# Conv taps as diagonal products, short convolutions' middle tap on ScalarE, decay masks added by TensorE

## The chip, the cores and the metric

The kernel runs on one core of one Trainium2 chip. The metric is the device time of one launch in microseconds (us). The engines are called TensorE (PE in the profile, its weight loads PEld), VectorE (DVE), ScalarE (ACT), GpSimd (POOL) and SyncE (SP, which issues most transfers). All engines take their own instructions in order and wait for each other through semaphores.

## What is computed

Two layers over 256 latent tokens and 256 context tokens of width 1024 (each layer two feed-forward parts around a mixer), then two further layers on the 256 latent tokens alone. The change touches only the first layer's "even" mixer. Cut to what matters:

```python
qkv, z, ab, glu = split(h @ w_in)                     # 512 tokens in all, latent and context
qkv = silu(depthwise_conv(qkv, qkv_conv))             # 5 taps, 1536 channels
q, k, v = split(qkv)                                  # 4 heads of 128 each
g, beta = gates(ab)                                   # per direction, token and head
# gated delta rule in both directions; within a chunk:
gcum  = cumsum(g)
decay = where(tril, exp(gcum[i] - gcum[j]), 0)        # upper triangle in the other direction
m     = strict(beta * k k^T * decay);  a = I + m      # triangular solve against v and k
attn  = tril(q k^T * decay)
val, gate = split(glu)
y = depthwise_conv(val * sigmoid(gate), dw_conv) + dw_bias   # 31 taps, 512 channels
y = silu(layer_norm(y))
out = concat(rms_norm(o) * silu(z), y) @ w_out
```

## The kernel before, in words

Nearly all weight products are made exact enough by splitting both operands into a high and a low part of a faster 32-bit form (`hi`, line 77, on ScalarE; `lo`, line 80, on VectorE) and adding three products (`mm3`, lines 111 to 113). Products that are not split are in plain F32: scores of keys and queries, state products, level products of the triangular inverse, the attention scores of the second layer (line 1153).

The mixer is `even` (lines 558 to 845) and `even_scan` (847 to 1046), then `mix_even`, the output product. `even` goes through the input projection in blocks of 128 channels by 512 tokens (`blocks`: 24 products into one of two banks of PSUM): gates and keys (four blocks, each with `conv5`, sum of squares and a transpose), decay tiles, inverse of the diagonal blocks, the gated input of the long convolution (stage `e_glu`, lines 782 to 795: four padded blocks `upad`), queries, values, and the `z` gate. Between blocks `ada_next` inserts one group of a conditioning product (line 229, whose weights come straight from memory). `even_scan` completes the inverse by levels (lines 861 to 902), steps the state over four token tiles in two directions (`step`), merges the directions (`merge`), does the long convolution (`conv31`, lines 998 to 1007) and its layer norm (`cnorm`).

Nothing fixes the order by hand: a planner orders the instructions of each engine by the order of the program text as priority, by readiness in its own estimate of time, and by free buffers. So instructions that stand late in the text, such as the taps of `conv31`, run early where their engine would be free. Tiles with the same tag share a fixed number of buffers, and a new one waits until the old one's last reader is done.

The places that the change and the prediction touch:

- `conv5` (line 593): ScalarE copies the product from its bank into a padded tile (597); VectorE multiplies by the first tap (602) and adds four more (604); ScalarE applies SiLU (607). It runs twelve times.
- Decay tiles (lines 730 to 750): for each of four token tiles and two directions, four transposes of a broadcast gate column (740) into a bank of role `ch` (two banks), each followed by a Relu on ScalarE (741), then one Exp (742), a multiply by a triangular mask of ones and zeros on VectorE (744), four multiplies (747) into a tile `un` (two buffers), which is stored to memory (749).
- `e_glu`: product of the gate block, sigmoid into the padded tile (791), product of the value block, multiply on VectorE (793).
- `conv31` for each of four blocks: the first tap with the bias (1005) and 30 further taps (1007), all on VectorE, into `y`.
- Bank 7 (role `pss`) holds the sums of squares, first of the keys, later of the queries.
- `un`, `pad`, `acc` live in the pool `ip`, which is freed after `even`; `upad`, `dm` and `y` live on.

Of the kernel before, what the change touches and what calls it, by code (L numbers as in the profile page):

```python
# [9 lines left out]
F32 = mybir.dt.float32  # L10
F32R = mybir.dt.float32r
I32 = mybir.dt.int32
AF = mybir.ActivationFunctionType
ALU = mybir.AluOpType
# [7 lines left out]
LN_EPS = 1e-5  # L22
RMS_EPS = 1e-6
NEG = -1.0e30


def shape_constants():
# [26 lines left out]
class Net:  # L54
# [503 lines left out]
    def even(self, xh, xl):  # L558
        nc, I = self.nc, self.I
        v = nc.vector  # L560
        W = I["even_w_in"][0].rearrange("(k p) n -> p k n", p=128)
        gd, ip = self.gd, self.ip
        qT = gd.tile([128, 4, 512], F32, name="qT")
        kT = gd.tile([128, 4, 512], F32, name="kT")
        y = self.yo.tile([128, 4, 512], F32, name="y")
# [5 lines left out]
        cw = self.cw  # L571

        def unit(c0):
            raw = self.raw()
            rv = raw.rearrange("p (k n) -> p k n", k=KC)
            nc.sync.dma_start(rv, W[:, :, c0:c0 + 256])
            return [self.split(rv[:, 4 * q:4 * q + 4, :]) for q in range(2)]

        def blocks(todo, cuts=((0, 512),)):

            out = [self.pt() for _ in todo]
            for a, b in cuts:
                for ps, lhs in zip(out, todo):
                    for k in range(KC):
                        wh, wl = lhs(k)
                        self.mm3(ps[:, a:b], wh, wl, xh[:, k, a:b], xl[:, k, a:b], k == 0, k == KC - 1)
            return out

        def col(pieces, j):
            c = slice(128 * j, 128 * j + 128)  # L590
            return lambda k: (pieces[k // 4][0][:, k % 4, c], pieces[k // 4][1][:, k % 4, c])

        def conv5(ps, blk, out=None):
            pad = ip.tile([128, 2, 260], F32, name="pad", tag="pad", bufs=2)
            nc.gpsimd.memset(pad[:, :, 0:2], 0.0)
            nc.gpsimd.memset(pad[:, :, 258:260], 0.0)
            nc.scalar.copy(pad[:, :, 2:258], ps.rearrange("p (s t) -> p s t", s=2))
            acc = ip.tile([128, 2, 256], F32, name="acc", tag="acc", bufs=3)
            for j in range(5):
                w = cw[:, 12 * j + blk:12 * j + blk + 1]  # L600
                if j == 0:
                    v.tensor_scalar(acc, pad[:, :, 0:256], w, None, op0=ALU.mult)
                else:
                    v.scalar_tensor_tensor(acc, pad[:, :, j:j + 256], w, acc, op0=ALU.mult, op1=ALU.add)
            fa = acc.rearrange("p s t -> p (s t)")
            out = fa if out is None else out
            nc.scalar.activation(out, fa, AF.Silu)
            return out
# [27 lines left out]
        ps, psk = blocks([lambda k: (wh[:, k, :], wl[:, k, :]), col(pieces, 0)], ((0, 256), (256, 512)))  # L636
        abf = ip.tile([128, 512], F32, name="abf", tag="acc", bufs=3)[:16]
        nc.scalar.copy(abf, ps[:16])
        ps = self.pt([128, 4, 16], "ch")
# [10 lines left out]
        def small(name, pool=None):  # L650
            return (pool or gd).tile([128, 2, 4, 4], F32, name=name)
# [7 lines left out]
        xa, ax, u, den, s, s2, g = (small(n, ip) for n in ("ga", "gx", "gu", "gn", "gs", "gt", "gg"))  # L659
# [31 lines left out]
        ps = self.pt([128, 64], "ch")  # L691
# [3 lines left out]
        gc, egc, negc, etail, egl = (small(n) for n in ("gc", "egc", "negc", "etail", "egl"))  # L695
# [11 lines left out]
        for h in range(4):  # L707
            if h == 2:
                pieces = unit(768)
            if h:  # L710
                psk, = blocks([col(pieces, h % 2)])
            c = conv5(psk, 4 + h)
            sumsq(c, h, pss)
            tokmajor(c, khat[:, :, h, :])
            if h % 2:
                self.ada_next()
        rk = gd.tile([128, 16], F32, name="rk")
        self.rsqrt(rk, pss.rearrange("p t h -> p (t h)"), 1e-6)
        for t in (2, 3, 0, 1):
            v.tensor_mul(khat[:, t], khat[:, t], rk[:, 4 * t:4 * t + 4, None].to_broadcast([128, 4, 128]))  # L720
            nc.sync.dma_start(kvd[t, :, 0], khat[:, t])
            ps = self.pt([128, 4, 128], "tp")
# [4 lines left out]
        self.mark("e_dm")  # L727

        dm = {}
        for t in (2, 3, 0, 1):  # L730
            ts = slice(128 * t, 128 * (t + 1))
            psg = self.pt([128, 4, 128], "tp")
            for h in range(4):
                nc.tensor.matmul(psg[:, h, :], kT[:, h, ts], kT[:, h, ts], start=True, stop=True)
            for d in range(2):
                psr = self.pt([128, 4, 128], "ch")
                e = gd.tile([128, 4, 128], F32, name="dm", tag="dm", bufs=8)
                for h in range(4):
                    cl = gc[:, d, t, h:h + 1]
                    nc.tensor.transpose(psr[:, h, :], cl.to_broadcast([128, 128]), self.ident)  # L740
                    nc.scalar.activation(e[:, h, :], psr[:, h, :], AF.Relu, scale=-1.0, bias=cl)
                nc.scalar.activation(e, e, AF.Exp, scale=-1.0)
                m = (self.le, self.ge)[d]
                v.tensor_mul(e, e, m[:, None, :].to_broadcast([128, 4, 128]))
                un = ip.tile([128, 4, 128], F32, name="un", tag="un", bufs=2)
                for h in range(4):
                    v.scalar_tensor_tensor(un[:, h, :], psg[:, h, :], nbeta[:, d, t, h:h + 1], e[:, h, :],
                                           op0=ALU.mult, op1=ALU.mult)
                nc.sync.dma_start(ud[d][4 * t:4 * t + 4].rearrange("h j i -> j h i"), un)
                dm[d, t] = e  # L750
# [3 lines left out]
        for d in range(2):  # L754
            z = gd.tile([128, 16, 128], F32, name=f"Z{d}")
# [27 lines left out]
        for b2 in range(2):  # L783
            pv, pg = unit(2064 + 256 * b2), unit(2576 + 256 * b2)
            for j in range(2):
                pad = gd.tile([128, 2, 286], F32, name=f"upad{2 * b2 + j}")
                nc.gpsimd.memset(pad[:, :, 0:15], 0.0)
                nc.gpsimd.memset(pad[:, :, 271:286], 0.0)
                psg, = blocks([col(pg, j)])
                core = pad[:, :, 15:271]  # L790
                nc.scalar.activation(core, psg.rearrange("p (s t) -> p s t", s=2), AF.Sigmoid)
                psv, = blocks([col(pv, j)])
                v.tensor_mul(core, core, psv.rearrange("p (s t) -> p s t", s=2))
                pads.append(pad)
                self.ada_next()

        self.mark("e_q")
# [2 lines left out]
        for h in range(4):  # L800
            if h % 2 == 0:
                pieces = unit(128 * h)
            ps, = blocks([col(pieces, h % 2)])
            conv5(ps, h, qT[:, h, :])
            sumsq(qT[:, h, :], h, pss)
            if h % 2:
                self.ada_next()
# [3 lines left out]
        for t in (2, 3, 0, 1):  # L811
            ts = slice(128 * t, 128 * (t + 1))
            ps = self.pt([128, 4, 128], "tp")
# [7 lines left out]
        for h in range(4):  # L821
            if h % 2 == 0:
                pieces = unit(1024 + 128 * h)
            ps, = blocks([col(pieces, h % 2)])
            c = conv5(ps, 8 + h)
            vt = ip.tile([128, 4, 128], F32, name="vt", tag="acc", bufs=3)
            tokmajor(c, vt)
            nc.sync.dma_start(kvd[:, :, 1, h, :].rearrange("t p c -> p t c"), vt)
            if h % 2:
                self.ada_next()  # L830
# [3 lines left out]
        for h in range(4):  # L834
            if h % 2 == 0:
                pieces = unit(1536 + 128 * h)
            ps, = blocks([col(pieces, h % 2)])
# [9 lines left out]
    def even_scan(self, E):  # L847


        nc = self.nc  # L850
        v = nc.vector
# [6 lines left out]
        y = E["y"]  # L858
# [139 lines left out]
        def conv31(b):  # L998
            self.mark("e_cf")
            acc = y[:, b, :].rearrange("p (s t) -> p s t", s=2)  # L1000
            pad = E["pads"][b]
            for i in range(31):
                w = self.dw[:, 4 * i + b:4 * i + b + 1]
                if i == 0:
                    v.tensor_scalar(acc, pad[:, :, 0:256], w, self.cf_bias[:, b:b + 1], op0=ALU.mult, op1=ALU.add)
                else:
                    v.scalar_tensor_tensor(acc, pad[:, :, i:i + 256], w, acc, op0=ALU.mult, op1=ALU.add)  # L1007


        def cnorm():  # L1010
# [30 lines left out]
        for b in range(4):  # L1041
            conv31(b)
# [221 lines left out]
    def hybrid(self, l, xs, last):  # L1264
# [3 lines left out]
        with tc.tile_pool(name="hb", bufs=1, reuse_waits="tile") as hb:  # L1268
# [10 lines left out]
            for i in (0, 2):  # L1279
                v.tensor_scalar(negc[:, i], self.ge, -NEG, NEG, op0=ALU.mult, op1=ALU.add)  # L1280
            causal = [negc[:, 0], negc[:, 1:3].rearrange("p a b -> p (a b)")]
# [75 lines left out]
            def select():  # L1357

                for t in range(2):
# [21 lines left out]
                    for i in range(8):  # L1381
                        v.max(m8, idx)
                        v.match_replace(idx, m8, idx, 3.0 * NEG)
                        yield
                    v.tensor_scalar(idx, idx, 2.0 * NEG, None, op0=ALU.is_le)
                    v.tensor_scalar(idx, idx, -NEG, NEG, op0=ALU.mult, op1=ALU.add)
                    v.tensor_tensor(idx, idx, causal[t], op=ALU.min)
# [418 lines left out]
```

## Time and profile before

| | |
|---|---|
| median of 3 runs | 2521.53 us (2517.78 to 2525.92) |
| the profiled execution | 2521.85 us |
| its span, first to last instruction | 2520.1 us |
| mean granted TensorE clock | 0.997 of full speed |
| even mixer with its output product | about 430 to 745 us of the span |

The profile gives for each engine its busy time, for groups of instructions their count and mean duration, and for idle time what ended it. A matmul's end is modelled, and neighbouring matmuls overlap in the record, so a busy TensorE need not be at its limit. Rows of stretches (windows) give the busy time of each engine between two times. In the timeline consecutive equal instructions are merged into one row, with their count.

### The profile page before, as it was taken

Reading aid. Unit: us, or ns where it says so; the run is one execution under the profiler, and the core shown is the slowest. Engines: PE = TensorE matmul, PEld = TensorE weight load, DVE = VectorE, ACT = ScalarE, POOL = GpSimd, SP = SyncE. Lnnn points to the kernel's source line nnn. Section 1 sums busy time; section 2 is a strip of 40 time slices with the busy share of each in tenths; the row PEclk is TensorE's granted clock in tenths of the full one; section 3 lists DMA queues with packets and bytes.
Section 4 is the critical chain, followed back from the end, with each engine's and each line's share of the span. In section 5 each row is a group of like instructions: output and inputs, shape, how many; then the busy total and the mean of one; then the engine's idle time right before and its main releaser. Section 6 shows DMA issues by size and latency. Waiting matters only on the chain.

```text
span 2520.1 us, 32989 instructions
## 1 busy us (share of the span) xinstructions
PE 2458.2 (98%) x13096; PEld 2003.7 (80%) x13096; DVE 1382.8 (55%) x2430; ACT 1049.0 (42%) x1764; POOL 38.2 (2%) x102
## 2 busy tenths in 40 slices
PE   7999999999999999999999999999999999999998
PEld 4777887767888888888788887589978878888776
DVE  3322245799887322346222346665576766657755
ACT  3322234723334222324222335654455564546544
POOL 0000001000000000000000000000000000000000
PEclk9999999999999999999999999999999999999999
DMA  8644333566535333225443324767655335553353
GB/s 281 215 150 134 134 101 134 170 204 235 199 110 193 91 100 101 101 95 189 154 130 100 118 97 167 275 205 214 192 175 181 102 134 192 176 172 113 126 180 142
DMA packets 342728, 395.76 MB, mean 157 GB/s; under 512 B 19464, under 2 KB 236845, under 8 KB 342573
## 3 DMA queue, kind: packets, MB, share of 16 engines
q1 hardware_dynamic: 342573, 393.64, 47.7%
q8 instruction: 103, 1.69, 0.3%
q14 instruction: 52, 0.43, 0.0%
HBM read 377.06 MB, written 16.55 MB: 156 GB/s over the span
## 4 chain that ended last, share of the span: by engine, by line
PE 74%; issue 13%; DVE 8%; DMA 2%; ACT 2%; POOL 1%; SPq 0%; DVEq 0%; POOLq 0%; ACTq 0%
PE b L111 21%; PE b L112 21%; PE b L113 21%; PE b L229 2%; PE b L301 1%; DVE wlo L80 1%; DVE y L1007 1%; PE b L1352 1%; DMA fraw<-in_ada_w 1%; DVE st L435 1%; DVE b L433 1%; PE b L1161 1%; DVE x L441 0%; DVE x L434 0%; PE b L235 0%
## 5 line engine op out<-in xcount | busy, mean ns | idle before, releaser
L80 DVE TENSOR_TENSOR wlo<-wraw,whi 128x1024 fp32r<-128x1024 f32 (+2 forms) x499 | 600.1, 1206 | 689.0 <-ACT whi L77 687.9
L77 ACT CAST whi<-wraw 128x1024 fp32r<-128x1024 f32 (+2 forms) x499 | 514.7, 1038 | 499.3 <-PE b L112 288.9
L111 PE MATMUL b<-xh,whi 128*128 128x512 f32 (+1 forms) x1688 | 607.3, 360 | 4.2 <-ACT xh L77 3.9
L113 PE MATMUL b<-xh,wlo 128*128 128x512 f32 (+1 forms) x1688 | 605.2, 359 | 3.1 <-DVE wlo L80 3.1
L112 PE MATMUL b<-xl,whi 128*128 128x512 f32 (+1 forms) x1688 | 606.7, 360 | 0.4 <-DVE xl L80 0.2
L111 PEld LDWEIGHTS b<-xh,whi 128*128 128x128 f32 x1688 | 319.6, 189 | 66.2 <-issue 10.9
L113 PEld LDWEIGHTS b<-xh,wlo 128*128 128x128 f32 x1688 | 320.1, 190 | 50.5 <-DVE wlo L80 4.8
L112 PEld LDWEIGHTS b<-xl,whi 128*128 128x128 f32 x1688 | 320.0, 190 | 46.8 <-issue 1.7
L111 PE MATMUL b<-whi,hh 128*128 128x512 f32 x652 | 254.5, 390 | 0.0
L113 PE MATMUL b<-whi,hl 128*128 128x512 f32 x652 | 254.3, 390 | 0.0
L112 PE MATMUL b<-wlo,hh 128*128 128x512 f32 x652 | 254.3, 390 | 0.0
L465 ACT ACTIVATE h<-b 128x512 f32<-128x512 f32 (+1 forms) x88 | 47.8, 544 | 321.1 <-PE b L113 321.0
L111 PE MATMUL b<-whi,x 128*128 128x512 f32 (+1 forms) x448 | 171.3, 383 | 0.8 <-ACT xtt L308 0.8
L113 PE MATMUL b<-whi,x 128*128 128x512 f32 (+1 forms) x448 | 171.1, 382 | 0.0
L112 PE MATMUL b<-wlo,x 128*128 128x512 f32 (+1 forms) x448 | 170.6, 381 | 0.0
L111 PEld LDWEIGHTS b<-whi,hh 128*128 128x128 f32 x652 | 122.4, 188 | 26.3
L113 PEld LDWEIGHTS b<-whi,hl 128*128 128x128 f32 x652 | 122.4, 188 | 26.1
L112 PEld LDWEIGHTS b<-wlo,hh 128*128 128x128 f32 x652 | 122.4, 188 | 25.9
L80 DVE TENSOR_TENSOR hl<-h,hh 128x512 fp32r<-128x512 f32 (+1 forms) x81 | 50.2, 621 | 150.3 <-ACT hh L77 150.3
L77 ACT CAST hh<-h 128x512 fp32r<-128x512 f32 (+1 forms) x81 | 45.9, 567 | 196.8 <-PE b L112 188.0
L111 PEld LDWEIGHTS b<-whi,x 128*128 128x128 f32 x448 | 84.2, 188 | 16.2 <-ACT xtt L308 1.0
L112 PEld LDWEIGHTS b<-wlo,x 128*128 128x128 f32 x448 | 84.2, 188 | 16.0 <-issue 1.5
(475 smaller groups left out, 3181.9 us busy)
## 6 DMA issues: line engine op xcount, KB each, us to landing
wraw<-in_ffn_w_gu SPq DMA_DIRECT2D x170, 512.0 KB, 4.8
fraw<-in_ada_w SPq DMA_DIRECT2D x64, 1024.0 KB, 6.4
wraw<-in_w_in SPq DMA_DIRECT2D x64, 1024.0 KB, 4.9
wraw<-in_ffn_w_down SPq DMA_DIRECT2D x44, 1024.0 KB, 4.8
wraw<-in_even_w_in SPq DMA_DIRECT2D x12, 1024.0 KB, 5.1
wraw<-in_w_branch SPq DMA_DIRECT2D x12, 1024.0 KB, 4.8
araw<-in_ada_w SPq DMA_DIRECT2D x8, 1024.0 KB, 7.9
xd<-x SPq DMA_DIRECT2D x16, 512.0 KB, 4.3
```

What stands on the lines that cost most here:

```text
L77: self.nc.scalar.copy(out, in_)
L80: return self.nc.vector.tensor_sub(out, in_, hi)
L111: mm(ps, ah, bh, start=start, stop=False)
L112: mm(ps, ah, bl, start=False, stop=False)
L113: mm(ps, al, bh, start=False, stop=stop)
L229: nc.tensor.matmul(ps[32 * q:32 * q + 32], self.sil[:, 4 * u + q, :], raw[:, q, :], start=(u == 0), stop=(u == 1))
L301: nc.tensor.transpose(ps[:, j, :], n[:, 128 * k:128 * (k + 1)], self.ident)
L433: nc.vector.tensor_mul(ys[n], ys[n], gate[:, c])
L435: nc.vector.bn_stats(st[:, n, :], x[:, c])
L465: nc.scalar.activation(h(c), ps[0], AF.Silu)
L1007: v.scalar_tensor_tensor(acc, pad[:, :, i:i + 256], w, acc, op0=ALU.mult, op1=ALU.add)
L1161: nc.tensor.matmul(po, vt[:, c, h // 4], pT[:, c], start=(c == 0), stop=(c == 3))
```

## The change

Three edits, all in the even mixer:

1. `conv5`: the middle tap (2) is made by ScalarE from the bank, as a copy with a per-channel scale straight into `acc`; VectorE adds the other four taps. The padded copy stays.
2. Decay tiles: two small tiles `low` (0 where the mask was one, -1e30 where it was zero) are made once. For each decay tile TensorE first writes the identity times the broadcast `low` over the whole bank and then adds the gate columns with four plain products in place of the transposes. Relu and Exp turn the masked places into zeros, so the multiply by the mask goes.
3. Long convolution: in `e_glu`, as soon as a padded block is there, ScalarE makes six diagonal matrices (identity times the tap's per-channel weight), in buffers of the tag `un`; TensorE adds up six products of a diagonal with the shifted block in bank 7; ScalarE writes the sum plus bias into `y`. `conv31` adds the other 25 taps on VectorE.

```diff
@@ -22,6 +22,7 @@
 LN_EPS = 1e-5
 RMS_EPS = 1e-6
 NEG = -1.0e30
+PT = 6
 
 
 def shape_constants():
@@ -596,12 +597,10 @@
             nc.gpsimd.memset(pad[:, :, 258:260], 0.0)
             nc.scalar.copy(pad[:, :, 2:258], ps.rearrange("p (s t) -> p s t", s=2))
             acc = ip.tile([128, 2, 256], F32, name="acc", tag="acc", bufs=3)
-            for j in range(5):
-                w = cw[:, 12 * j + blk:12 * j + blk + 1]
-                if j == 0:
-                    v.tensor_scalar(acc, pad[:, :, 0:256], w, None, op0=ALU.mult)
-                else:
-                    v.scalar_tensor_tensor(acc, pad[:, :, j:j + 256], w, acc, op0=ALU.mult, op1=ALU.add)
+            w = lambda j: cw[:, 12 * j + blk:12 * j + blk + 1]
+            nc.scalar.activation(acc, ps.rearrange("p (s t) -> p s t", s=2), AF.Copy, scale=w(2))
+            for j in (0, 1, 3, 4):
+                v.scalar_tensor_tensor(acc, pad[:, :, j:j + 256], w(j), acc, op0=ALU.mult, op1=ALU.add)
             fa = acc.rearrange("p s t -> p (s t)")
             out = fa if out is None else out
             nc.scalar.activation(out, fa, AF.Silu)
@@ -727,6 +726,10 @@
         self.mark("e_dm")
 
         dm = {}
+        low = ip.tile([128, 2, 128], F32, name="low").rearrange("p d f -> d p f")
+        low = [low[d] for d in range(2)]
+        for z, m in zip(low, (self.le, self.ge)):
+            v.tensor_scalar(z, m, -NEG, NEG, op0=ALU.mult, op1=ALU.add)
         for t in (2, 3, 0, 1):
             ts = slice(128 * t, 128 * (t + 1))
             psg = self.pt([128, 4, 128], "tp")
@@ -735,13 +738,17 @@
             for d in range(2):
                 psr = self.pt([128, 4, 128], "ch")
                 e = gd.tile([128, 4, 128], F32, name="dm", tag="dm", bufs=8)
+
+                nc.tensor.matmul(psr, self.ident, low[d][:, None, :].to_broadcast([128, 4, 128]),
+                                 start=True, stop=False)
                 for h in range(4):
                     cl = gc[:, d, t, h:h + 1]
-                    nc.tensor.transpose(psr[:, h, :], cl.to_broadcast([128, 128]), self.ident)
+                    nc.tensor.matmul(psr[:, h, :], cl.to_broadcast([128, 128]), self.ident,
+                                     start=False, stop=(h == 3))
+                for h in range(4):
+                    cl = gc[:, d, t, h:h + 1]
                     nc.scalar.activation(e[:, h, :], psr[:, h, :], AF.Relu, scale=-1.0, bias=cl)
                 nc.scalar.activation(e, e, AF.Exp, scale=-1.0)
-                m = (self.le, self.ge)[d]
-                v.tensor_mul(e, e, m[:, None, :].to_broadcast([128, 4, 128]))
                 un = ip.tile([128, 4, 128], F32, name="un", tag="un", bufs=2)
                 for h in range(4):
                     v.scalar_tensor_tensor(un[:, h, :], psg[:, h, :], nbeta[:, d, t, h:h + 1], e[:, h, :],
@@ -792,6 +799,17 @@
                 psv, = blocks([col(pv, j)])
                 v.tensor_mul(core, core, psv.rearrange("p (s t) -> p s t", s=2))
                 pads.append(pad)
+
+                b = 2 * b2 + j
+                dg = [ip.tile([128, 4, 128], F32, name="dg", tag="un", bufs=2) for _ in range(0, PT, 4)]
+                dg = [dg[i // 4][:, i % 4] for i in range(PT)]
+                ps = self.pt([128, 2, 256], bank=7)
+                for i in range(PT):
+                    nc.scalar.activation(dg[i], self.ident, AF.Copy, scale=self.dw[:, 4 * i + b:4 * i + b + 1])
+                for i in range(PT):
+                    nc.tensor.matmul(ps, dg[i], pad[:, :, i:i + 256], start=(i == 0), stop=(i == PT - 1))
+                nc.scalar.activation(y[:, b, :].rearrange("p (s t) -> p s t", s=2), ps, AF.Identity,
+                                     bias=self.cf_bias[:, b:b + 1])
                 self.ada_next()
 
         self.mark("e_q")
@@ -999,12 +1017,9 @@
             self.mark("e_cf")
             acc = y[:, b, :].rearrange("p (s t) -> p s t", s=2)
             pad = E["pads"][b]
-            for i in range(31):
+            for i in range(PT, 31):
                 w = self.dw[:, 4 * i + b:4 * i + b + 1]
-                if i == 0:
-                    v.tensor_scalar(acc, pad[:, :, 0:256], w, self.cf_bias[:, b:b + 1], op0=ALU.mult, op1=ALU.add)
-                else:
-                    v.scalar_tensor_tensor(acc, pad[:, :, i:i + 256], w, acc, op0=ALU.mult, op1=ALU.add)
+                v.scalar_tensor_tensor(acc, pad[:, :, i:i + 256], w, acc, op0=ALU.mult, op1=ALU.add)
 
 
         def cnorm():
```

## Rows read from the trace of the kernel before

**Rows 1.** The page: busy time of each engine; the chain that ended last.

```profile
PE 2458.2 (98%) x13096; PEld 2003.7 (80%) x13096; DVE 1382.8 (55%) x2430; ACT 1049.0 (42%) x1764; POOL 38.2 (2%) x102
...
PE 74%; issue 13%; DVE 8%; DMA 2%; ACT 2%; POOL 1%; SPq 0%; DVEq 0%; POOLq 0%; ACTq 0%
```

**Rows 2.** Stretches: length, then each engine's busy us (x), clock, DMA share, GB/s.

```profile
430.00:745.00 315.00, 303.64 (x1965) 239.33 (x1964) 273.40 (x608) 134.57 (x250) 7.40 (x24) 0.99 0.56 184
...
505.00:627.00 122.00, 117.09 (x614) 84.94 (x612) 117.52 (x241) 39.36 (x56) 0.80 (x12) 0.99 0.67 216
560.00:580.00 20.00, 17.53 (x99) 14.04 (x98) 17.47 (x38) 7.58 (x10) 0.27 (x4) 0.91 0.64 211
840.00:860.00 20.00, 20.00 (x90) 16.57 (x89) 6.27 (x6) 5.41 (x6) 0.00 (x0) 1.00 0.31 90
```

**Rows 3.** Timeline of TensorE, 505.18 to 506.31 us: start us, us, instruction.

```profile
505.18 0.39 PE L113 MATMUL b<-xh,wlo 128*128 128x512 f32 x1
505.40 0.39 PE L111 MATMUL b<-xh,whi 128*128 128x512 f32 x1
...
506.31 0.39 PE L112 MATMUL b<-xl,whi 128*128 128x512 f32 x1
```

**Rows 4.** TensorE by line and shape, 505 to 627 us: count | busy us, mean ns | idle.

```profile
L112 PE MATMUL b<-xl,whi 128*128 128x512 f32 x123 | 49.5, 403 | 0.0
L111 PE MATMUL b<-xh,whi 128*128 128x512 f32 x123 | 49.5, 402 | 0.3 <-ACT whi L77 0.3
L113 PE MATMUL b<-xh,wlo 128*128 128x512 f32 x123 | 48.8, 400 | 3.1 <-DVE wlo L80 3.1
L229 PE MATMUL b<-fraw,sil 128*32 128x512 f32 x128 | 16.0, 601 | 0.0
L815 PE MATMUL b<-qT,kT 128*128 128x128 f32 x32 | 4.8, 282 | 0.8 <-ACT qT L607 0.8
...
L870 PE MATMUL b<-cst,Z 128*128 128x128 f32 x9 | 1.4, 279 | 0.0
```

**Rows 5.** Chain of waits, 580 to 600 us: start us, us, what.

```profile
582.93 1.85 PE b L229 x16
```

**Rows 6.** Timeline of TensorE, 1585 to 1590 us (second layer's attention).

```profile
1585.49 0.59 PE L1153 MATMUL b<-kT,qT 128*128 128x512 f32 x1
...
1587.60 1.88 PE L1153 MATMUL b<-kT,qT 128*128 128x512 f32 x4
```

**Rows 7.** Timeline of TensorE, 632 to 640 us (products and transposes of the levels).

```profile
633.94 3.74 PE L880 MATMUL b<-Z,lv 128*128 128x128 f32 x32
637.51 1.91 PE L870 MATMUL b<-cst,Z 128*128 128x128 f32 x16
```

**Rows 8.** Groups by line, 430 to 745 us: count | busy us, mean ns | idle.

```profile
L1007 DVE SCALAR_TENSOR_TENSOR y<-upad,vd,y 128x512 f32<-128x512 f32 x120 | 85.6, 743 | 0.1
...
L880 PE MATMUL b<-Z,lv 128*128 128x128 f32 x128 | 14.9, 275 | 0.0
...
L919 ACT ACTIVATE st<-kv,etail 128x128 f32<-128x128 f32 x24 | 8.5, 402 | 16.5 <-DMA kv<-kvd 8.3 <-issue 5.2 <-PE b L938 3.0
...
L597 ACT COPY pad<-b 128x512 f32<-128x512 f32 x12 | 7.0, 585 | 23.5 <-PE b L113 23.5
...
L602 DVE TENSOR_SCALAR acc<-pad,vw 128x512 f32<-128x512 f32 x12 | 5.8, 480 | 4.3 <-ACT pad L597 4.2
...
L744 DVE TENSOR_TENSOR dm<-dm,cst 128x512 f32<-128x512 f32 x8 | 5.2, 684 | 0.2 <-ACT dm L742 0.2
```

**Rows 9.** Waits of TensorE, 430 to 745 us: us in total, times, longest.

```profile
PE b L113 <- DVE wlo L80: 3.1, 2, 1.6
...
PE b L815 <- ACT qT L607: 0.8, 1, 0.8
```

**Rows 10.** Line 1007 by stretch: length, VectorE's busy us (x), clock, DMA share, GB/s.

```profile
505.00:627.00 122.00, 62.76 (x90) 0.99 0.67 216
627.00:680.00 53.00, 17.82 (x25) 1.00 0.68 232
```

## The prediction, made blind

> **What bounds the kernel now.** The page first [rows 1]: TensorE is busy 98% of the span, and three quarters of the chain that ended last lies on it. VectorE is busy 55% over all, ScalarE 42%. A share over the whole span hides stages, so the second view is the busy time by stretch. The three edits lie between about 430 us (the key convolutions) and 745 us (the mixer's output product). In those 315 us TensorE is busy 303.64 us: 11.4 us of visible idle [rows 2]. In the middle part, 505 to 627 us, VectorE is busy 117.52 of 122 us, more than anywhere else, and TensorE 117.09. So two engines stand at the brim there, and the question is which of them really sets the pace.
>
> Busy time can't answer it, because a matmul's record is longer than its place in the queue. The product of the split weights (128x512, lines 111 to 113) has a record of 0.39 us, yet the starts in the timeline follow each other by (506.31 - 505.18) / 5 = 0.226 us [rows 3]. So I count instead. In 505 to 627 us there are 123 records on each of the three lines: 369 x 0.226 = 83.4 us. The 128 records of line 229 are eight groups of 16, and one group holds the chain for 1.85 us: 14.8 us. The other 117 records (from line 815 to line 870, none wider than 128 columns) take at most 0.112 each, as worked out below: 13.1 us. Sum 111.3 of 122 [rows 4, 5]. TensorE has at most 10.7 us to spare there: 4.9 visible, the rest in gaps too short to be seen.
>
> By contrast, the Trainium skill (Perfetto Trace Analysis, section Identifying the Most-Contended Engine) says that matmul busy time is a bad measure of TensorE's headroom and that the share of weight loads is a good one. By it TensorE is 85 / 122 = 70% loaded in the middle part, with 37 us to spare, and the added products would fit. This case's rows disagree: where the products run back to back without a gap (840 to 860 us), weight loads are busy 16.57 of 20 us [rows 2], 83%, so that share never says "full" here.
>
> **The change, part by part.** Each product is in plain F32, not in the split form. Its price in the trace is the attention score at line 1153 (also 128x128 by 128x512): four records last from 1587.60 for 1.88 us, and the last of them 0.59, so the starts are (1.88 - 0.59) / 3 = 0.43 us apart [rows 6]. There are 32 records for 16 calls in the code, so one product holds TensorE for 0.86 us. For 128 columns: (3.74 - 0.28) / 31 = 0.112 us a record, two records a product; a transpose of the same size is one record, (1.91 - 0.28) / 15 = 0.109 [rows 7, 8].
>
> Long convolution on TensorE. Four channel blocks x 6 taps = 24 products: 24 x 0.86 = 20.6 us of TensorE, all in the projection stage, where every microsecond of TensorE is on the path but for the idle counted above. VectorE loses four first taps (taken as the multiply of line 602, 0.48 us) and 20 taps of 0.743 us: 4 x 0.48 + 20 x 0.743 = 16.8 us. ScalarE gets 24 diagonals (nearest row: copy with a scale, 128x128, line 919, 0.40 us) and four evacuations (0.59 us, line 597): 9.7 + 2.4 = 12.1 us [rows 8]. ScalarE was busy 39 of 122 us in the middle part [rows 2], so this lies beside other work; if that cover is gone (a diagonal issued only when its product is next), it costs what the second rival below costs.
>
> Decay masks. Eight tiles, each with one product of the identity with the mask, 128x512: 8 x 0.86 = 6.9 us of TensorE. The 32 transposes become plain products: 32 x (2 x 0.112 - 0.109) = 3.7 us. VectorE loses eight multiplies of 0.684 us, 5.5 us, and gets two small ones for the mask (at most 0.48 each). The ScalarE work per tile is unchanged, but the first Relu now waits for the last of the five products instead of its own transpose; with two banks for these tiles the next tile's products lie beside this tile's Relus. I cost the wait at nothing.
>
> Short convolutions. Twelve multiplies leave VectorE, 12 x 0.48 = 5.8 us, and twelve scaled copies of 0.59 us come to ScalarE, 7.0 us. The bank is held one copy longer; the other bank covers that while a block's 24 products (24 x 0.226 = 5.4 us) run. Cost on the path: nothing.
>
> Sum on TensorE: 20.6 + 6.9 + 3.7 = 31.2 us more work in the stretch. VectorE has 27 us less.
>
> **What comes back.** A lighter VectorE can return no more than TensorE's waits. Visible idle in the whole stretch is 11.4 us, invisible gaps in the middle part 5.8 more. Certain candidates: products waiting for a split on VectorE (line 113 on line 80), 3.1 us; the scores' wait for a convolved query, 0.8 us [rows 9]. Behind those waits the granted clock in 560 to 580 us averages 0.91 [rows 2], which means a part of it was spent at 1.2 GHz instead of 2.4 GHz: 0.09 x 20 = 1.8 us. After 627 us, 17.8 us of taps lie between the steps of the state scan [rows 10]. Now VectorE's other work in the middle part is 117.5 - 62.8 - 8 x 0.48 = 51 us, and 100 remaining taps at 0.70 (90 took 62.76) are 70 us: 121 us, and the middle part will be some 15 to 20 us longer than 122. So the taps end before the scan, and its hand-offs get shorter; of the 6.5 us of visible idle that lie outside the middle part I take a third, 2 us. Returned: 3.1 + 0.8 + 1.8 + 2 = 7.7 us. Against it stands about half a microsecond of new waiting; the net is 7. Bounds: nothing returned, or all of the visible idle, the short gaps and the clock, 11.4 + 5.8 + 1.8 = 19 us.
>
> The profiled execution took 2521.85 us (span 2520.1), 0.3 us from the median of the runs, 2521.53, so no correction. 2521.9 + 31.2 - 7 = 2546.1, said as 2546 us, 1.0% slower. A measurement of this kernel can tell about 0.3%, 7.6 us, from no change.
>
> **Rivals.**
> *VectorE sets the pace, and the kernel gets faster.* Place: 505 to 627 us. If the products of TensorE only wait for splits behind taps, the part shortens by what VectorE loses in it, 16.8 + 8 x 0.48 = 20.6 us: 2501 us. For it: VectorE at 96%, and the longest waits of TensorE are for VectorE. Against it: it needs 20.6 + 20.6 = 41 us of room on TensorE, and the count leaves 10.7. It decides if the products' true spacing were under 0.15 us. By the rule of the skill's page named above, whose 37 us come near that room, this would be the outcome. 4%.
> *The idle swallows nearly all.* Short gaps also exist before 505 and after 627 us, where I did not count them; if they amount to another 10 us and all is filled, 2521.9 + 31.2 - 29 = 2524 us, no difference. 5%.
> *The products come cheaper.* If a product with a diagonal took one record at 0.226 us, the form of the split weights, 32 of them would add 7.2 us, with the transposes 10.9: 2526 us, no difference. Against it: both operands are plain F32, and all such rows show two records. 4%.
> *A new wait.* The diagonals use the two buffers of the tile that the decay stage stores to memory, so each block's diagonals wait for the block before it (or, for the first, for the stores); all blocks also share one bank. If the planner puts products into TensorE's queue before ScalarE has made them, each block waits for its six diagonals, 4 x 6 x 0.40 = 9.6 us, with the splits and projections queued behind: 2546 + 10 = 2556 us. For it: TensorE takes its queue in order. Against: ScalarE is two thirds idle there. 15%.
>
> **How the numbers follow.** The forecast, 2546, has 72%. Its bounds are 2521.9 + 31.2 - 19 = 2534 and 2553. The order of all instructions is planned anew, so I add a few microseconds below, and the new wait above: 2532 to 2560 us. Left out are the three cheap cases (13%) and the tails. Faster by over 0.3%: the first rival, 4%. Within 0.3%: 5 + 4 = 9%. Slower: 87%.
>
> **What would show it.** In the profile of the changed kernel: 48 records of the new conv products 0.43 us apart, 16 of the mask product, 64 in place of 32 on the gate columns; taps 100 instead of 124, the last before the state scan's first step; TensorE's visible idle in this stretch about 5 us; the stretch longer by 24 us, and everything behind it shifted by as much and not changed. The forecast is wrong if the new records stand under 0.3 us apart, if the stretch grows by less than 12 us, or if TensorE shows long waits for the diagonals.

## The result and the profile after

The changed kernel takes 2545.24 us (median of 4 runs, 2542.61 to 2547.47) against 2522.26 us for the kernel before beside it. The ratio is 1.0093, 95% interval 1.0080 to 1.0105: 23.4 us slower. The profiled execution took 2545.96 us, its span is 2544.2 us.

Line numbers have moved: in the changed kernel the products with diagonals are on line 810, the mask products on 742, the gate columns on 746, the remaining taps on 1022, and the split-weight products on 112 to 114.

Stretches of the changed kernel first; columns as in [rows 2]. The mixer now runs over 20 us longer, so 430 to 769 stands against 430 to 745 before (both end inside the output product), 505 to 653 against 505 to 627, and 584 to 604 is the neighbourhood in which the clock dipped before.

```profile
430.00:769.00 339.00, 333.87 (x2057) 254.97 (x2057) 253.88 (x566) 151.53 (x289) 6.41 (x24) 1.00 0.52 171
505.00:653.00 148.00, 148.00 (x712) 100.42 (x714) 130.87 (x254) 55.99 (x89) 0.80 (x12) 1.00 0.59 195
584.00:604.00 20.00, 20.00 (x121) 16.01 (x122) 16.86 (x31) 7.50 (x12) 0.27 (x4) 1.00 0.45 158
```

Visible idle of TensorE fell from 11.4 to 5.1 us. In the middle part there is none left, 148.00 of 148, while VectorE is down to 130.87 of 148, 88% against 96% before: it stands idle for 17.1 us there, against 4.5 before, although taps from later stretches have moved in. Weight loads are busy 100 of 148 us, 68%, a little less than the 70% before, although TensorE is fuller than before: the longer F32 products have one load per 0.43 us. So that share said nothing about the room in either kernel.

Where the middle part ends can be read from the last SiLU of the `z` gate, line 839 before and line 857 after (count, min/median/max duration in ns, first and last start):

```profile
L839 ACT ACTIVATE zs<-b x4: 591/598/600, 612.5 to 625.9; 128x512 f32<-128x512 f32 x4
```
```profile
L857 ACT ACTIVATE zs<-b x4: 594/600/604, 639.3 to 652.6; 128x512 f32<-128x512 f32 x4
```

It comes 26.7 us later. The last record of the output product, which ends the mixer, is on line 113 before and 114 after:

```profile
L113 PE MATMUL b<-wsp,hl x32: 389/389/494, 744.2 to 777.0; 128*128 128x512 f32 x32
```
```profile
L114 PE MATMUL b<-wsp,hl x32: 389/389/499, 766.9 to 799.0; 128*128 128x512 f32 x32
```

It comes 22.0 us later, so levels, scan and output product gave 4.7 us back. At the end of the span the shift is 24.1 us: another 2.1 came up behind the mixer, where nothing was changed.

The new instructions, by line (count, busy us, mean ns, idle before):

```profile
L810 PE MATMUL b<-upad,dg 128*128 128x512 f32 x48 | 21.7, 600 | 1.2 <-ACT dg L808 1.2
L746 PE MATMUL b<-cst,gc 128*128 128x128 f32 x64 | 9.2, 276 | 0.0
L742 PE MATMUL b<-low,cst 128*128 128x512 f32 x16 | 8.3, 599 | 0.0
L601 ACT ACTIVATE acc<-b,vw 128x512 f32<-128x512 f32 x12 | 8.2, 683 | 0.0
L808 ACT ACTIVATE dg<-cst,vd 128x128 f32<-128x128 f32 x24 | 7.8, 391 | 18.8 <-PE b L810 16.5 <-DMA ud<-un 2.3
L811 ACT ACTIVATE y<-b,vg 128x512 f32<-128x512 f32 x4 | 2.8, 689 | 7.6 <-PE b L810 7.6
```

The counts are those forecast: 48, 16 and 64 records. The spacing is in the timeline of TensorE:

```profile
465.39 1.05 PE L746 MATMUL b<-cst,gc 128*128 128x128 f32 x8
...
501.29 5.40 PE L810 MATMUL b<-upad,dg 128*128 128x512 f32 x12 [1.19 <-ACT dg L808]
```

Twelve records of one block fill 5.40 us: (5.40 - 0.59) / 11 = 0.437 us apart, and eight gate columns (1.05 - 0.28) / 7 = 0.11. So the added work on TensorE is 48 x 0.437 + 16 x 0.43 + (64 x 0.11 - 32 x 0.109) = 21.0 + 6.9 + 3.6 = 31.5 us. The span grew by 24.1, so 7.4 us came back. The mixer alone grew by 23.4 us, since its first small product for the gates (line 641 before, 640 after) started at 435.35 us before and at 434.00 after, and its last record comes 22.0 us later; so counted, 8.1 us came back.

The waits of TensorE over 430 to 770 us (us in total, times, longest); the two left out are 0.4 and 0.3 us:

```profile
PE b L810 <- ACT dg L808: 1.2, 1, 1.2
PE b L230 <- DVE fm L238: 0.7, 1, 0.7
PE b L944 <- DVE st L945: 0.7, 1, 0.7
PE b L977 <- DVE st L951: 0.7, 1, 0.7
PE b L893 <- ACT lv L889: 0.6, 1, 0.6
```

The waits for a split and for a convolved query of [rows 9] are gone. The one new wait, 1.2 us for the first block's diagonals, is all that shows of sharing buffers with the decay stage: line 808 above stood idle for 2.3 us until the stage's stores had landed. The remaining taps, in the middle part, columns as in [rows 10]:

```profile
505.00:653.00 148.00, 72.43 (x100) 1.00 0.59 195
```

All 100 taps lie before the level products and the scan. Before, 25 of them stood behind 627 us; of their 17.8 us, 11.3 lay among the levels and 6.5 behind 655 us, where the scan's first product starts (line 938, 655.1 us).

### The profile page after: what moved, and what is told of

Read it like the earlier page. It is cut to its first block, busy times and chain, and to the rows that moved or that the text cites. A ratio compares the mean times of both kernels' runs of the same rounds, so it can differ in the third digit from the quotient of the medians.

```text
span 2544.2 us, 33214 instructions
## 1 busy us (share of the span) xinstructions
PE 2486.3 (98%) x13192; PEld 2017.3 (79%) x13192; DVE 1363.3 (54%) x2388; ACT 1066.9 (42%) x1805; POOL 36.9 (1%) x102
## 4 chain that ended last, share of the span: by engine, by line
PE 76%; issue 13%; DVE 5%; DMA 3%; ACT 2%; POOL 1%; SPq 0%; DVEq 0%; POOLq 0%; ACTq 0%
PE b L112 22%; PE b L114 21%; PE b L113 21%; PE b L230 3%; PE b L810 1%; DMA araw<-in_ada_w 1%; DVE wlo L81 1%; PE b L302 1%; PE b L1367 1%; PE b L236 1%; DVE st L436 1%; DVE x L435 1%; DVE b L434 0%; DMA wraw<-in_w_in 0%; PE b L1168 0%
```

## The experiments

The kernel before ran again beside each group of four kernels: 2520.93 us (median of 23 runs) beside the first four, 2519.37 us (median of 17) beside the last four. I compare by ratios, and turn a ratio into microseconds with 2522. The executions of one kernel differ by 4 to 14 us, and the longer ones mostly have the lower mean clock: among the 23, 2517.13 us came with 0.998 and 2529.67 us with 0.995.

**The edits one by one.** The first takes only edit 1 into the kernel before:

```diff
-            for j in range(5):
-                w = cw[:, 12 * j + blk:12 * j + blk + 1]
-                if j == 0:
-                    v.tensor_scalar(acc, pad[:, :, 0:256], w, None, op0=ALU.mult)
-                else:
-                    v.scalar_tensor_tensor(acc, pad[:, :, j:j + 256], w, acc, op0=ALU.mult, op1=ALU.add)
+            w = lambda j: cw[:, 12 * j + blk:12 * j + blk + 1]
+            nc.scalar.activation(acc, ps.rearrange("p (s t) -> p s t", s=2), AF.Copy, scale=w(2))
+            for j in (0, 1, 3, 4):
+                v.scalar_tensor_tensor(acc, pad[:, :, j:j + 256], w(j), acc, op0=ALU.mult, op1=ALU.add)
```

Expected:

> Only the short convolutions' middle tap is made on ScalarE; decay masks and long convolution as before. TensorE gets no work, VectorE loses 5.8 us. If TensorE sets the pace (my theory): only a part of its waits for VectorE returns, 0 to 3 us, so 2519 to 2522 us. If VectorE sets the pace: the 5.8 us come back nearly whole, 2516 us.

Measured: 2516.52 us, ratio 0.9982 (0.9971 to 0.9994), 4.5 us faster. That is nearer to the rival's 5.8 us than to my 0 to 3, but the interval, 1.5 to 7.3 us, takes in most of both, so alone it decides nothing. Its profile shows a part of what was returned: TensorE's visible idle is 8.2 us (430 to 740 us) against 11.4, the dip of the clock that stood at 560 to 580 us in [rows 2] is missing (1.00), and TensorE is busy 19.42 of 20 us there instead of 17.53.

```profile
560.00:580.00 20.00, 19.42 (x123) 14.41 (x123) 17.04 (x41) 8.38 (x12) 0.27 (x4) 1.00 0.68 237
```

The second takes only the decay masks:

```diff
...
+                nc.tensor.matmul(psr, self.ident, low[d][:, None, :].to_broadcast([128, 4, 128]),
+                                 start=True, stop=False)
...
-                    nc.tensor.transpose(psr[:, h, :], cl.to_broadcast([128, 128]), self.ident)
+                    nc.tensor.matmul(psr[:, h, :], cl.to_broadcast([128, 128]), self.ident,
+                                     start=False, stop=(h == 3))
...
-                v.tensor_mul(e, e, m[:, None, :].to_broadcast([128, 4, 128]))
```

Expected:

> Only the decay masks are added by TensorE. TensorE gets 8 x 0.86 + 32 x (2 x 0.112 - 0.109) = 10.6 us, VectorE loses 5.5 us at a place where it is busy 55 of 75 us. My theory: the whole of the 10.6 us less at most 1 us, 2532 us. If VectorE sets the pace: 2517 us.

Measured: 2533.43 us, ratio 1.0050 (1.0031 to 1.0068), 12.6 us slower, where 10.6 less 1 was forecast. The interval, 7.8 to 17.1 us, holds the forecast, so neither an extra cost nor a return of VectorE's 5.5 us is shown; a faster kernel, as the rival wanted, is excluded. The profiled executions are only 9.1 us apart (spans of 2529.2 and 2520.1 us). In this one the stall that cost clock before is here too, and the mean clock of its twenty microseconds is 0.83, against 0.91 in [rows 2]: (0.91 - 0.83) x 20 = 1.6 us, already within the 9.1. The two longest of the six executions, 2536.80 and 2537.17 us, are the two with the lowest mean clock, 0.995 and 0.994.

```profile
550.00:570.00 20.00, 16.18 (x71) 12.29 (x70) 16.38 (x27) 5.83 (x9) 0.13 (x2) 0.83 0.58 199
```

The third takes only the six taps of the long convolution:

```diff
...
+                for i in range(PT):
+                    nc.scalar.activation(dg[i], self.ident, AF.Copy, scale=self.dw[:, 4 * i + b:4 * i + b + 1])
+                for i in range(PT):
+                    nc.tensor.matmul(ps, dg[i], pad[:, :, i:i + 256], start=(i == 0), stop=(i == PT - 1))
...
-            for i in range(31):
+            for i in range(PT, 31):
...
```

Expected:

> Only the six taps of the long convolution go to TensorE. TensorE gets 24 x 0.86 = 20.6 us, VectorE loses 16.8 us. My theory: 20.6 less some 4 to 6 us of waits that go, 2537 to 2539 us. If VectorE sets the pace: 2505 us.

Measured: 2534.53 us, ratio 1.0051 (1.0032 to 1.0071), 12.9 us slower. So 20.6 - 12.9 = 7.7 us came back, 2 to 4 more than I said, which the interval, 8.1 to 17.9 us, can't tell from the forecast; the 17 us that VectorE was relieved of did not come back. The three edits alone add up to -4.5 + 12.6 + 12.9 = 21.0 us, against 23.4 together. The interval of each is about 3 to 5 us to either side, so they may be additive; that is not shown.

**VectorE's relief without TensorE's work.** The kernel before, with the work only taken away from VectorE:

```diff
-            for j in range(5):
+            for j in range(4):
...
-                v.tensor_mul(e, e, m[:, None, :].to_broadcast([128, 4, 128]))
...
-            for i in range(31):
+            for i in range(6, 31):
...
```

Expected:

> The kernel before with VectorE's work left out and put nowhere: taps 0 to 5 of the long convolution, the last tap of the short ones and the decay masks' multiply (these parts of the computation are missing). VectorE loses 24 x 0.743 + 12 x 0.743 + 8 x 0.684 = 32 us, TensorE and ScalarE keep their work. My theory: this shows what a lighter VectorE returns by itself, about 8 us and at most 19: 2514 us (2503 to 2520). If VectorE sets the pace: the 24 us that lie in the middle part, 2498 us.

Measured: 2514.65 us, ratio 0.9975 (0.9962 to 0.9987), 6.3 us faster. This run speaks most plainly against the rival: 32 us less work on the engine that was busy 96% of the middle part buys 6 us. It is also an estimate of the most that a version of this change could win, if its work on TensorE were free. Its mixer, 430 to 738 us, and the middle part:

```profile
430.00:738.00 308.00, 301.16 (x1963) 237.30 (x1964) 247.38 (x561) 133.43 (x250) 6.41 (x24) 1.00 0.56 188
505.00:620.00 115.00, 112.75 (x590) 82.23 (x590) 110.67 (x228) 36.08 (x52) 0.80 (x12) 1.00 0.73 244
```

TensorE's visible idle is 6.8 us of 308, against 11.4 of 315. VectorE is still busy 110.67 of 115 us, 96%: taps that stood later have moved up into the room. So its share didn't fall, and yet the part is shorter: a full VectorE is no sign that it sets the pace. Alone the run doesn't exclude that those taps still hold up splits, but TensorE has only 2.3 us of visible idle left in the part, and the runs with more and with cheaper products below settle it. About half of the 6.3 us looks like clock. The mean granted clock was 0.9967 over the 23 executions of the kernel before and 0.9979 over the 11 of this one; if TensorE set the pace in that time, 0.0012 x 2521 = 3 us, an estimate.

**TensorE's work without VectorE's relief.** The changed kernel with VectorE's work put back:

```diff
-            for j in (0, 1, 3, 4):
+            for j in (0, 1, 2, 3, 4):
...
+                v.tensor_mul(e, e, m[:, None, :].to_broadcast([128, 4, 128]))
...
-            for i in range(PT, 31):
+            for i in range(31):
```

Expected:

> The changed kernel with VectorE's work put back beside TensorE's: all 31 taps, all five short taps and the mask multiply run on VectorE as well (taps 0 to 5 and the middle tap are thus added twice, the mask is applied twice). TensorE has its 31 us more, VectorE nothing less. My theory: 31.2 us and nothing returned, about 2552 us, 7 us above the changed kernel. If the gain were hidden in VectorE's work (VectorE sets the pace wherever TensorE does not), it would be slower by the 32 us put back, 2577 us.

Measured: 2556.27 us, ratio 1.0147 (1.0132 to 1.0162), 37.1 us slower than before. Nothing is returned, as expected, but it is 6 us more than the 31.2 that I took for TensorE's work. Its profile has one stretch that the others lack:

```profile
732.00:742.00 10.00, 9.82 (x76) 9.28 (x76) 6.18 (x26) 1.10 (x3) 0.00 (x0) 0.50 0.00 0
```

For 10 us, at the end of the levels and in the first steps of the scan, TensorE was granted 1.2 GHz, half of its clock: at most 5 us lost, which would close the sum. The four executions bear this out: two took 2552.96 and 2552.75 us, at a mean clock of 0.997 and 0.999, which is the forecast of 2552; the other two, the profiled one among them, took 2559.58 and 2562.03 us, at 0.995 and 0.996. From 700 to 732 us TensorE had been busy 29.74 us, at full clock. Why the clock fell in this kernel's scan and not in the others' was not tried.

**More taps.** Twelve taps, diagonals made four at a time in the same two buffers:

```diff
-PT = 6
+PT = 12
...
+                for i0 in range(0, PT, 4):
+                    dg = ip.tile([128, 4, 128], F32, name="dg", tag="un", bufs=2)
```

Expected:

> The changed kernel with twelve taps instead of six as products, the diagonals made four at a time. My theory: each further tap costs 4 x 0.86 us on TensorE, and VectorE's relief has nothing left to return: 24 x 0.86 = 20.6 us more, 2565 us (2560 to 2568). If six taps were just under the point from which the relief pays, or if their cost were a fixed wait per block: 2550 us or less.

Measured: 2563.92 us, ratio 1.0177 (1.0163 to 1.0191), 44.6 us slower than before, 21.2 more than six taps. So from six taps to twelve each tap costs TensorE's price in full, 0.86 us a block, within the noise (20.6 us by price), and up to twelve there is no point from which the relief begins to pay.

**Cheaper products.** The changed kernel with the same diagonals, buffers and bank, but the products in the short 32-bit form; the low parts are left out, so these six taps are less exact:

```diff
-                dg = [ip.tile([128, 4, 128], F32, name="dg", tag="un", bufs=2) for _ in range(0, PT, 4)]
+                dg = [ip.tile([128, 4, 128], F32R, name="dg", tag="un", bufs=2) for _ in range(0, PT, 4)]
...
+                padr = ip.tile([128, 2, 261], F32R, name="padr")
+                self.hi(padr, pad[:, :, 0:261])
...
-                    nc.tensor.matmul(ps, dg[i], pad[:, :, i:i + 256], start=(i == 0), stop=(i == PT - 1))
+                    nc.tensor.matmul(ps, dg[i], padr[:, :, i:i + 256], start=(i == 0), stop=(i == PT - 1))
```

Expected:

> The changed kernel with the six products per block in the short 32-bit form (diagonal and a rounded copy of the block, low parts left out, so the six taps lose precision): one record of 0.226 us in place of two of 0.43 us; ScalarE gets one more copy of 0.6 us per block; diagonals, buffers, bank and waits as they were. My theory: 24 x (0.86 - 0.226) = 15.2 us less, 2530 us. If the cost lay in waiting for diagonals, buffers or the bank: 2543 us or more.

Measured: 2527.38 us, ratio 1.0033 (1.0022 to 1.0045): 8.3 us slower than before, and 15.1 less than the changed kernel, 1.0093 - 1.0033. Its timeline has six records per block:

```profile
511.71 1.57 PE L812 MATMUL b<-padr,dg 128*128 128x512 f32 x6
```

With a record of 0.39 us at the end, (1.57 - 0.39) / 5 = 0.24 us a product. The block still waits for its diagonals and shares its buffers; only the time on TensorE is shorter. So these 15 us of the taps' cost are TensorE's time and no wait.

**Relief that costs TensorE nothing.** The kernel before with edit 1, and the masks' multiply on GpSimd:

```diff
...
-                v.tensor_mul(e, e, m[:, None, :].to_broadcast([128, 4, 128]))
+                nc.gpsimd.tensor_mul(e, e, m[:, None, :].to_broadcast([128, 4, 128]))
```

Expected:

> The kernel before with the short convolutions' middle tap on ScalarE and the decay masks' multiply on GpSimd: work only leaves VectorE, none comes to TensorE. My theory: the relief of VectorE is worth at most some 6 us in all and the middle tap has returned 4 of them: 2513 to 2517 us. If the eight slower multiplies (128x512 on GpSimd took 1.5 us in the state scan) delay the decay tiles: 2520 us or more.

Measured: 2515.77 us, ratio 0.9985 (0.9976 to 0.9993). That is 3.8 us faster (1.8 to 6.1), within the forecast. It beats both kernels, but not edit 1 alone (0.9982), from which it can't be told apart: nothing is seen of the masks' share of the relief. The multiplies took 1.46 us each on GpSimd:

```profile
L742 POOL TENSOR_TENSOR dm<-dm,cst 128x512 f32<-128x512 f32 x8 | 11.7, 1464 | 25.5 <-ACT dm L740 25.5
```

A part of their cost falls on VectorE. While two of them ran, VectorE's four multiplies of the normalised keys, which take 0.683 us each in the kernel before (line 720), took up to 1.78 us:

```profile
478.75 4.66 DVE L718 TENSOR_TENSOR khat<-khat,rk 128x512 f32<-128x512 f32 x4
478.87 3.39 POOL L742 TENSOR_TENSOR dm<-dm,cst 128x512 f32<-128x512 f32 x2 [3.67 <-ACT dm L740]
```

TensorE waited 1.3 us in two places for these keys, which it doesn't in the kernel before, so some of the masks' relief was probably taken back. Edit 1 alone, the smaller of the two changes, is the version to keep.

## Why the prediction was right

The forecast was 2546 us, with 31.2 us of new work on TensorE and 7 us net returned. Measured: 2545.24 us, 31.5 us of work by the changed kernel's own rows, and 7.4 us returned in the profiled execution, 8.1 by the mixer alone. That the forecast came within 1 us is partly luck: the interval of the ratio alone is 20 to 26 us, and the single edits were missed by 1 to 5 us.

*Which engine sets the pace.* Counting records by their spacing, in place of their durations, left 10.7 us of room in a middle part where both engines stood near the brim. The run with VectorE's relief alone (6.3 us for 32) and the one with twelve taps (21.2 us for six more) show it from both sides, and the run in the short form shows that TensorE's time is what counts. For the first of these runs the rival with VectorE at the pace wanted 2498 us where 2514.65 was measured, and for the change itself 2501 us. The rival in which idle swallows nearly all wanted 2524 us.

*The price of a product.* 0.43 us per record, read from the second layer's attention, came out as 0.437, in 48 records; the rival with one record of 0.226 us a product falls. The run in the short form moved by 15.1 us where 15.2 was worked out.

*What came back.* The terms 3.1 (split) and 0.8 us (query) are gone from the list of waits. The clock's 1.8 us came back in the profiled execution: 0.91 in [rows 2], 1.00 in the row of 584 to 604 us. The levels and the scan were forecast to return 2 us because the taps end before them; they do, and behind the middle part TensorE's visible idle fell by 2.5 us, from 6.3 (627 to 745 us) to 3.8 (653 to 769 us). In all, visible idle gave 11.4 - 5.1 = 6.3 us and the clock 1.8, together 8.1 us, which is also what the mixer's length shows. The prediction read [rows 10] wrongly in one point: most of the 25 taps behind 627 us stood among the levels, not between the steps of the scan.

*The middle part's length* was put some 15 to 20 us over 122 us. Its end moved by 26.7; probably the masks' 10.6 us, before 505 us, also push it: I named both terms but didn't add them at this point. Nothing in the sum hung on it.

*The new wait* (15%) exists, but only for the first block: 1.2 us of the 9.6 that four blocks would have cost. The other blocks' products stood late enough in TensorE's queue: it shows no wait for their diagonals.

*ScalarE at no cost* held: it was busy 151.53 of 339 us, and TensorE waited for it 1.2 us (the diagonals) and 0.6 us, although two of its copies were dearer than I took them (below).

Less exact were the single edits: I gave edit 1 at most 3 us of return (4.5 measured), the masks 2532 us (2533.43), the taps 2537 to 2539 us (2534.53). Edits 1 and 3 returned 4.5 and 7.7 us alone, and all three together 7.4: probably they draw on the same few waits, and whichever comes alone gets them; that was not tried further. VectorE's busy time fell by 19.5 us in the mixer, 273.40 to 253.88, not by the 27 worked out; why is not shown, and nothing in the sum hung on it.

## What to carry to other kernels

When two engines are both near 100%, price the move by the engine that receives the work: take the spacing of its records in a dense stretch, multiply by the counts, and see what room is left; here it was at most 10.7 us for 31. What the relieved engine can return is bounded by the waits and the idle of the engine that sets the pace, with the clock that it loses behind them, and a run that simply leaves the work out measures that bound, in the order then planned, before any of the new code is written. Of an edit in three parts, try the one that loads only an idle engine by itself: here it was worth 4.5 us and the other two lost some 25.

## What the hardware showed that I had not expected

A copy from PSUM to SBUF on ScalarE with a scale or a bias per channel took 0.683 and 0.689 us for 128x512 (lines 601 and 811 above), a plain copy of the same size 0.585 us [rows 8]. I had priced all three alike. By the Trainium skill (ScalarE: Activation LUTs, section What ACT_TABLE_LOAD costs) each operand of scale or bias that is read from memory per channel adds about 93 ns; the 98 and 104 ns here agree with it. The plain copy is another instruction (COPY, not ACTIVATE); against the SiLU of line 857 above, an ACTIVATE of the same size without such an operand, 0.600 us, it is 83 and 89 ns.

In three of the profiled kernels the granted clock fell to 1.2 GHz inside the mixer: in the kernel before (0.50 in 570 to 572 us), with the masks alone (0.50 in 560 to 564 us), and with VectorE's work put back (0.50 in 732 to 742 us). In the first two TensorE had just waited: 1.47 us for a split, until 567.93 us, in the kernel before; 1.66 us for a convolved query and 1.17 us for a split, until 558.57 us, with the masks alone. So a short wait could cost more than its own length: in the kernel before, 0.09 x 20 = 1.8 us on top of the waits. Whether the waits were the cause was not tried.

A dip of the same size stands in the second layer of the kernel before (0.91 in 1540 to 1560 us), which no edit touches, and the changed kernel's profile has none there or later. So two profiled executions can differ by some 2 us for this alone, and a difference of that size between their spans need not come from an edit.
